# NSA attention branches of a transformer block: two of four heads' exponentials weighted on ScalarE in place of GpSimd

## The chip, the cores and the metric

One core of one Trainium2 chip runs the whole block as one program. The metric is the device time of one execution in microseconds (us). TensorE does the matmuls and transposes, VectorE (DVE in the profile) and ScalarE (ACT) work on SBUF and PSUM, GpSimd (POOL) on SBUF only, SyncE (SP) issues DMAs.

## The reference, cut to what matters

The block takes x (1024 tokens by 1024), projects it, runs two attentions (an NSA attention with three branches and a sliding-window attention with a sink), mixes them with gates, projects, and ends with an MLP. The change touches two branches of the NSA attention, "selected" and "window". For 2 groups of 4 heads, in 8 blocks of 128 queries, each branch computes

```python
e = jnp.exp(s - m)                                   # masked_softmax
p = e / jnp.maximum(jnp.sum(e, axis=-1, keepdims=True), 1e-30)
o_s = jnp.einsum('bgrqn,bgqnd->bqgrd', p_s, vg)       # selected branch
o_w = jnp.einsum('bgrqk,bkgd->bqgrd', p_w, vwc)       # window branch
return gs[..., 0:1] * oc + gs[..., 1:2] * o_s + gs[..., 2:3] * o_w
```

so a row of exponentials of one head is divided by its sum and multiplied by its gate: one factor per query (partition) and head. With 16 blocks of 64 keys in all and 16 to be chosen, the selected branch takes every earlier key.

## The kernel before, in words

All matmuls with full-size operands are made of three (high by high, high by low, low by high), since each float32 operand is split into two float32r parts. The helper `split` (L84) does that: a copy on ScalarE (L87) writes the high part, a subtraction on VectorE or GpSimd (L91) the low part.

The NSA stage stands in `nsa_units` (L635). A unit is one branch of one query block: for each group g (2) and block i (8) a window unit (rows of up to 640 keys, L687 to L702) and a selected unit (rows of 128 times i + 1 keys, up to 1024, L705 to L722). That makes 32 units in all. A unit has two parts.

- `scores` (L478): for each of 4 heads, two matmuls per chunk of keys into a PSUM bank (L489, L490), a VectorE instruction that adds the bias, negates and keeps the running minimum (L496), and an Exp on ScalarE that also sums (L502). Then `weights` makes one factor per query and head in three small VectorE instructions (L646 to L648, the last one multiplying by the gate). Last, the four rows are multiplied in place by their factors: heads 1 and 3 on GpSimd (L510), heads 0 and 2 on VectorE (L513). `POOL_N` (L42) holds the heads for GpSimd; the sliding-window stage has `POOL_S` (L41), all four.
- `attend` (L516): per 128 keys, four transposes on TensorE into a PSUM bank `pt` (L520), a split of it into `th` (ScalarE, L87) and `tl` (VectorE, L91), and two matmuls into the output bank, with `th` (L532) and `tl` (L533). `fill` (L414) puts matmuls of the gate projections (L124 to L126, tile `mm`) behind the transposes. Those projections have splits of weights of their own, with the low part on GpSimd (`wl`, L91), and evictions on ScalarE (`gst`, L205).

`merge` and `run` (L535, L549) interleave the `attend` steps of one unit with the `scores` steps of the next. The compressed branch (tile `ec`, L656 to L675) goes in front of each window unit. The order of the instructions on each engine is not the program's own: L1267 opens the program with `schedule_with_timeline_sim=True`, so a planner orders them when the program is built, by its own estimate of when each is ready. On the chip each engine then runs its list in that order.

Of the kernel before, what the change touches and what calls it, by code (L numbers as in the profile page):

```python
# [10 lines left out]
AF = mybir.ActivationFunctionType  # L11
# [5 lines left out]
T = 1024  # L17
# [15 lines left out]
HEAD = (0.5, 0, 0.25, 0, 0, 0, 0, 0)  # L33
# [5 lines left out]
FILL_S = 2.0  # L39
FILL_N = 1.0  # L40
POOL_S = (0, 1, 2, 3)  # L41
POOL_N = (1, 3)  # L42
TB = 2
NPAIR = 16
NPRE = 4
# [7 lines left out]
def tile_hybrid_block(ctx: ExitStack, tc: tile.TileContext, x, norm_mix_pre, norm_mix_post, norm_mlp_pre,  # L53
                      norm_mlp_post, w_in, cmp_pos_k, cmp_w1_k, cmp_w2_k, cmp_pos_v, cmp_w1_v, cmp_w2_v,
                      attn_sinks, rel_bias, w_up_nsa, w_up_swa, w_out, w_mlp_in, w_mlp_out, onehot, out):
    nc = tc.nc
# [3 lines left out]
    def pool(name, bufs=1, side="left", space=None):  # L60
        kw = {} if space is None else {"space": space}
        if space is not DRAM:
            kw["reuse_waits"] = "tile"
        if space is None:
            kw["side"] = side
        return tc.tile_pool(name=name, bufs=bufs, **kw)
# [74 lines left out]
    def rstd_of(tp, ss):  # L141


        s = tp.tile([P, 1], F32, name="rs_s", tag="rs_s", bufs=3)
        nc.scalar.activation(s, ss, AF.Sqrt, scale=0.25 / D, bias=eps_t)
        t = tp.tile([P, 1], F32, name="rs_t", tag="rs_t", bufs=3)
        nc.vector.tensor_scalar(t, ss, 0.25 / D, 0.25 * EPS, op0=ALU.mult, op1=ALU.add)
        r = tp.tile([P, 1], F32, name="rs_r", tag="rs_r", bufs=3)
        nc.vector.reciprocal(r, s)
        a = tp.tile([P, 1], F32, name="rs_a", tag="rs_a", bufs=3)  # L150
        nc.vector.scalar_tensor_tensor(a, r, t, s, op0=ALU.mult, op1=ALU.add)
        o = tp.tile([P, 1], F32, name="rs_o", tag="rs_o", bufs=3)
        nc.vector.reciprocal(o, a)
        return o
# [17 lines left out]
    with ExitStack() as s_u:  # L172
# [36 lines left out]
        with ExitStack() as s:  # L209
# [33 lines left out]
            with ExitStack() as s0:  # L243
# [28 lines left out]
                for b in range(NB):  # L272
# [11 lines left out]
                    r = rstd_of(tp, ss)  # L284
# [115 lines left out]
        with ExitStack() as s:  # L400
# [13 lines left out]
            def fill(amount, after=None):  # L414

                credit[0] += amount
                while credit[0] >= 1.0:
                    credit[0] -= 1.0
                    done[0] += 1
                    if after is None:  # L420
                        step()
                    else:
                        with tc.issue_after(after.ins):
                            step()
# [27 lines left out]
            def q_proj(qp, c0, tag, bufs):  # L452
                res = []
                for _ in q_steps(qp, c0, tag, bufs, res):
                    pass
                return res
# [18 lines left out]
                        nc.vector.tensor_tensor(kl[other, cs], kf[own, :], kh[own, cs].bitcast(F32), op=ALU.subtract)  # L475
                return res

            def scores(ep, etag, ew, qs, qcol, chunks, inits, res, weights, on_pool, extra=0.0):  # L478


                nm = ep.tile([P, 4], F32, name="nm", tag="nm", bufs=4)
                sm = ep.tile([P, 4], F32, name="sm", tag="sm", bufs=4)
                n = sum(c[2] for c in chunks)
                for r in range(4):
                    e = ep.tile([P, ew], F32, name="e", tag=etag, bufs=4)
                    prev, off = inits[r], 0
                    for ci, (kh, kl, w, bias) in enumerate(chunks):
                        ps = ps_s()
                        nc.tensor.matmul(ps[:, :w], qs[r][:, qcol], kh, start=True, stop=False)  # L489
                        mm = nc.tensor.matmul(ps[:, :w], qs[r][:, qcol], kl, start=False, stop=True)  # L490
                        fill(extra, mm)
                        if ci == len(chunks) - 1:
                            acc = nm[:, r:r + 1]
                        else:
                            acc = ep.tile([P, 1], F32, name="nm0", tag="nm0", bufs=4)
                        nc.vector.tensor_tensor_reduce(out=e[:, off:off + w], in0=ps[:, :w], in1=bias(r), scale=-1.0,  # L496
                                                       scalar=prev, op0=ALU.add, op1=ALU.min, accum_out=acc)
                        prev = acc
                        off += w
                        if ci < len(chunks) - 1:  # L500
                            yield
                    nc.scalar.activation(e[:, :n], e[:, :n], AF.Exp, scale=-1.0, bias=nm[:, r:r + 1],  # L502
                                         accum_out=sm[:, r:r + 1])
                    res.append(e)
                    if r < 3:
                        yield
                w = weights(nm, sm)
                for r in range(4):
                    if r in on_pool:
                        nc.gpsimd.tensor_tensor(res[r][:, :n], res[r][:, :n], w[:, r:r + 1].to_broadcast([P, n]),  # L510
                                                op=ALU.mult)
                    else:
                        nc.vector.tensor_scalar(res[r][:, :n], res[r][:, :n], w[:, r:r + 1], None, op0=ALU.mult)  # L513
                yield
# [59 lines left out]
            with ExitStack() as s0:  # L574
                qp = s0.enter_context(pool("swa"))
# [47 lines left out]
            with ExitStack() as s0:  # L623
                qp = s0.enter_context(pool("nsa"))
                for g in range(2):
# [4 lines left out]
                    qs = q_proj(qp, C_QN + g * 256, "q", 4)  # L630
                    qs = qs + q_proj(qp, C_QN + g * 256 + 128, "q", 4)
# [3 lines left out]
                    def nsa_units():  # L635
                        for i in range(NB):
                            qc = slice(i * P, (i + 1) * P)
                            kend = (i + 1) * P
                            y0 = 896 - P * i
                            ones = [1e30] * 4  # L640
                            o = []

                            def weights(br, i=i):
                                def f(nm, sm):
                                    w = qp.tile([P, 4], F32, name="w", tag="wgt", bufs=4)
                                    nc.vector.tensor_scalar(w, sm, 1e-30, None, op0=ALU.max)  # L646
                                    nc.vector.reciprocal(w, w)
                                    nc.vector.tensor_tensor(w, w, gsig[:, i, br, g * 4:g * 4 + 4], op=ALU.mult)  # L648
                                    return w
                                return f  # L650
# [3 lines left out]
                            ew = []  # L654
# [22 lines left out]
                            if i < 4:  # L677
                                k0 = 0
                                chunks = [(kwh[:, 0:kend], kwl[:, 0:kend], kend,
                                           lambda r, y0=y0: bn[:, r, y0:])]  # L680
                            else:
                                k0 = (i - 4) * P
                                k1 = k0 + 256
                                chunks = [(kwh[:, k0:k1], kwl[:, k0:k1], 256, lambda r: bfar[:, r, :]),
                                          (kwh[:, k1:kend], kwl[:, k1:kend], 384, lambda r: bn[:, r, 640:])]

                            def scores_a(i=i, qc=qc, ew=ew, chunks=chunks, cmp_scores=cmp_scores, weights=weights):  # L687
                                cmp_scores()
                                yield
                                yield from scores(qp, "ew", 640, qs, qc, chunks, ones, ew, weights(2), POOL_N, HEAD[i])  # L690

                            def attends_a(i=i, k0=k0, ec=ec, ew=ew, o=o):
                                o.append(ps_o())
# [3 lines left out]
                                for kb in range(k0 // P, i + 1):  # L697
                                    attend(qp, ew, kb * P - k0, P, o[0], vn[:, kb, 2 + g].rearrange("p a d -> p (a d)"),
                                           False, False, FILL_N)
                                    yield  # L700

                            yield scores_a(), 1 + 4 * len(chunks), attends_a(), i + 2 - k0 // P  # L702


                            chunks = []  # L705
                            n = kend if i < 4 else kend // 2
# [3 lines left out]
                            es = []  # L710

                            def attends_b(i=i, es=es, o=o):
                                for kb in range(i + 1):
                                    attend(qp, es, kb * P, P, o[0], vn[:, kb, g].rearrange("p a d -> p (a d)"),
                                           False, kb == i, FILL_N)
                                    if kb < i:
                                        yield
                                put_o(o[0], g * 256, i)
                                yield

                            yield (scores(qp, "es", T, qs, qc, chunks, ones, es, weights(1), POOL_N, HEAD[i]), 4 * len(chunks),
                                   attends_b(), i + 1)  # L722

                    run(nsa_units(), 1)
            s_pv.close()
            s_ot = ctx.enter_context(ExitStack())
# [13 lines left out]
    with ExitStack() as s:  # L740
# [58 lines left out]
        ep = s_e.enter_context(pool("etmp"))  # L799
# [472 lines left out]
```

## Time and profile before

| what | value |
|---|---|
| time, 3 runs | 1577.01 us median, 1576.17 to 1580.71 |
| the profiled execution's own time | 1580.5 us |
| its span in the profile | 1578.7 us |
| mean granted clock of TensorE | 0.981 of full speed |
| busy: TensorE, VectorE, ScalarE, GpSimd | 94%, 69%, 48%, 28% of the span |

The time of an execution is a little longer than the span, which runs from the first instruction to the last. Times in the rows are us from the start of the span, durations of single instructions in the views by line are ns. In a row of the timeline, a bracket gives the time the engine was idle just before, and what ended that; "x2" means that two instructions are merged in one row. NSA units run between 300 and 690 us.

### The profile page before, as it was taken

What the parts mean: (1) busy time and instruction counts of PE and PEld (TensorE: products, weight loads), DVE (VectorE), ACT (ScalarE), POOL (GpSimd) and SP (SyncE); (2) the same over time, 40 slices, a digit from 0 to 9 for tenths busy, and PEclk for the clock granted to TensorE, in tenths of its full rate; (3) what the DMA queues carried; (4) which work ended last, traced back from release to release, by engine and by line L of the source; (5) the groups of instructions that cost most, each with busy time, mean ns of one, the idle gap of its engine ahead of it and who ended that gap; (6) DMA issues with size and microseconds to landing.
All of it is one profiled execution on the core that took longest, in us unless ns stands there. A gap on an engine that the chain in (4) does not pass through costs nothing. (4 is left out here: it accounts for less than half of the span.)

```text
span 1578.7 us, 20103 instructions
## 1 busy us (share of the span) xinstructions
PE 1487.3 (94%) x6920; PEld 1214.2 (77%) x6920; DVE 1088.4 (69%) x2086; ACT 751.2 (48%) x1461; POOL 439.8 (28%) x354
## 2 busy tenths in 40 slices
PE   6998999999899999999988978999999899999997
PEld 5897888878777777778866766778888688888886
DVE  5455775598964998836537787877757566594775
ACT  5343675576653766653336563332222334334543
POOL 3000351132310232231133014867555410000302
PEclk9999999999999999999999998999999999999999
DMA  7733125111132111164256652444443598263451
GB/s 201 256 103 82 38 51 154 41 44 31 34 97 51 47 34 31 34 225 139 94 186 229 225 159 58 158 162 156 147 153 134 208 336 302 94 188 118 150 184 54
DMA packets 162038, 204.79 MB, mean 130 GB/s; under 512 B 15120, under 2 KB 105264, under 8 KB 161936
## 3 DMA queue, kind: packets, MB, share of 16 engines
q1 hardware_dynamic: 154224, 180.68, 36.5%
q0 software_dynamic: 6992, 20.48, 3.7%
q10 hardware_dynamic: 720, 2.36, 0.4%
q8 instruction: 54, 0.88, 0.2%
q14 instruction: 48, 0.39, 0.1%
HBM read 153.02 MB, written 58.32 MB: 134 GB/s over the span
## 5 line engine op out<-in xcount | busy, mean ns | idle before, releaser
L124 PE MATMUL mm<-uh,wh 128*128 128x512 f32 x464 | 201.4, 434 | 4.1 <-DVE qb L448 3.2
L510 POOL TENSOR_TENSOR e<-e,w 128x256 f32<-128x256 f32 (+7 forms) x128 | 111.6, 898 | 286.4 <-DVE w L648 148.9
L125 PE MATMUL mm<-ul,wh 128*128 128x512 f32 x464 | 184.9, 398 | 0.0
L126 PE MATMUL mm<-uh,wl 128*128 128x512 f32 x464 | 184.5, 398 | 0.0
L87 ACT ACTIVATE th<-pt 128x512 fp32r<-128x512 f32 (+1 forms) x178 | 105.1, 593 | 95.0 <-PE pt L520 84.9
L502 ACT ACTIVATE e<-e,nm 128x256 f32<-128x256 f32 (+7 forms) x192 | 124.4, 649 | 36.8 <-DVE nm L496 36.4
L91 DVE TENSOR_TENSOR tl<-pt,th 128x512 fp32r<-128x512 f32 x162 | 110.0, 682 | 33.8 <-ACT th L87 32.7
L87 ACT ACTIVATE fh<-fraw 128x1024 fp32r<-128x1024 f32 x56 | 59.4, 1062 | 145.3 <-PE xs L1165 78.3
L87 ACT ACTIVATE wh<-wraw 128x1024 fp32r<-128x1024 f32 x69 | 73.0, 1058 | 111.1 <-PE mm L125 36.7
L91 DVE TENSOR_TENSOR fl<-fraw,fh 128x1024 fp32r<-128x1024 f32 x56 | 69.2, 1241 | 78.2 <-ACT fh L87 78.2
L520 PE MATMUL pt<-ident,e 128*128 128x128 f32 x648 | 104.8, 276 | 1.9 <-DVE e L513 0.9
L1165 PE MATMUL xs<-vl,fh 128*128 128x512 f32 x256 | 100.7, 393 | 4.2 <-DVE vl L91 4.2
L126 PEld LDWEIGHTS mm<-uh,wl 128*128 128x128 f32 x464 | 88.0, 190 | 20.9
L124 PEld LDWEIGHTS mm<-uh,wh 128*128 128x128 f32 x464 | 88.9, 192 | 17.4 <-issue 3.3
L91 DVE TENSOR_TENSOR wl<-wraw,wh 128x1024 fp32r<-128x1024 f32 x53 | 69.0, 1301 | 45.9 <-ACT wh L87 45.5
L1165 PE MATMUL xs<-vh,fl 128*128 128x512 f32 x256 | 100.5, 393 | 0.0
L1165 PE MATMUL xs<-vh,fh 128*128 128x512 f32 x256 | 100.2, 392 | 0.0
L1188 POOL TENSOR_TENSOR cc<-cc,gB 128x512 f32<-128x512 f32 x14 | 24.3, 1759 | 269.0 <-ACT sq L1187 267.3
L520 PEld LDWEIGHTS pt<-ident,e 128*128 128x128 f32 x648 | 81.7, 141 | 22.7 <-issue 2.5
L125 PEld LDWEIGHTS mm<-ul,wh 128*128 128x128 f32 x464 | 89.0, 192 | 12.0
L116 POOL TENSOR_TENSOR wl<-wraw,wh 128x384 fp32r<-128x384 f32 (+2 forms) x26 | 38.7, 1493 | 161.7 <-ACT wh L108 161.7
L91 POOL TENSOR_TENSOR wl<-wraw,wh 128x1024 fp32r<-128x1024 f32 x16 | 38.6, 2410 | 159.5 <-ACT wh L87 159.5
(286 smaller groups left out, 4086.0 us busy)
## 6 DMA issues: line engine op xcount, KB each, us to landing
fraw<-f_d SPq DMA_DIRECT2D x48, 512.0 KB, 3.6
wraw<-in_w_mlp_in_dram SPq DMA_DIRECT2D x36, 512.0 KB, 4.5
wraw<-in_w_out_dram SPq DMA_DIRECT2D x32, 512.0 KB, 3.6
f_d<-q SPq DMA_DIRECT2D x64, 256.0 KB, 3.6
b<-in_w_mlp_out_dram SPq DMA_DIRECT2D x32, 512.0 KB, 10.8
wraw<-in_w_in_dram SPq DMA_DIRECT2D x27, 512.0 KB, 4.7
f_d<-c SPq DMA_DIRECT2D x48, 256.0 KB, 4.0
gate_d<-gst SPq DMA_DIRECT2D x32, 256.0 KB, 2.1
```

Source lines behind the costliest of these rows:

```text
L87: nc.scalar.activation(h, src, AF.Copy)
L91: eng.tensor_tensor(l, src, h.bitcast(F32), op=ALU.subtract)
L116: eng.tensor_tensor(lv[:, a:b], rv[:, a:b], hv[:, a:b].bitcast(F32), op=ALU.subtract)
L124: nc.tensor.matmul(ps, ah, bh, start=first, stop=False)
L125: nc.tensor.matmul(ps, ah, bl, start=False, stop=False)
L126: nc.tensor.matmul(ps, al, bh, start=False, stop=last)
L502: nc.scalar.activation(e[:, :n], e[:, :n], AF.Exp, scale=-1.0, bias=nm[:, r:r + 1], accum_out=sm[:, r:r + 1])
L510: nc.gpsimd.tensor_tensor(res[r][:, :n], res[r][:, :n], w[:, r:r + 1].to_broadcast([P, n]), op=ALU.mult)
L520: tr = nc.tensor.transpose(pt[:rows, r, :], es[r][:, off:off + rows], ident)
L1165: nc.tensor.matmul(bank[t], l_[:, j, ts], r_[:, j, :], start=a_, stop=z_, skip_group_check=True)
L1188: (nc.vector if b == NB - 1 else nc.gpsimd).tensor_tensor(cc[:, ns], cc[:, ns], gB[:, ns], op=ALU.mult)
```

## The change

`scores` gets a second set, `on_act`. A head in it is multiplied on ScalarE as a Copy whose scale is the factor of each partition. The two calls in the NSA stage pass heads 1 and 3 there and nothing for GpSimd; the call in the sliding-window stage still passes its four heads for GpSimd.

```diff
-POOL_N = (1, 3)
+ACT_N = (1, 3)
...
-            def scores(ep, etag, ew, qs, qcol, chunks, inits, res, weights, on_pool, extra=0.0):
+            def scores(ep, etag, ew, qs, qcol, chunks, inits, res, weights, on_pool=(), extra=0.0, on_act=()):
...
                 w = weights(nm, sm)
                 for r in range(4):
-                    if r in on_pool:
+                    if r in on_act:
+                        nc.scalar.activation(res[r][:, :n], res[r][:, :n], AF.Copy, scale=w[:, r:r + 1])
+                    elif r in on_pool:
                         nc.gpsimd.tensor_tensor(res[r][:, :n], res[r][:, :n], w[:, r:r + 1].to_broadcast([P, n]),
                                                 op=ALU.mult)
                     else:
...
-                                yield from scores(qp, "ew", 640, qs, qc, chunks, ones, ew, weights(2), POOL_N, HEAD[i])
+                                yield from scores(qp, "ew", 640, qs, qc, chunks, ones, ew, weights(2), extra=HEAD[i], on_act=ACT_N)
...
-                            yield (scores(qp, "es", T, qs, qc, chunks, ones, es, weights(1), POOL_N, HEAD[i]), 4 * len(chunks),
+                            yield (scores(qp, "es", T, qs, qc, chunks, ones, es, weights(1), extra=HEAD[i], on_act=ACT_N), 4 * len(chunks),
                                    attends_b(), i + 1)
```

## Rows read from the trace of the kernel before

**Rows 1.** The page: TensorE over the whole span (busy us, share, instructions).
```profile
PE 1487.3 (94%) x6920; PEld 1214.2 (77%) x6920; DVE 1088.4 (69%) x2086; ACT 751.2 (48%) x1461; POOL 439.8 (28%) x354
```

**Rows 2.** Busy time by stretch: the NSA stage, then what follows it.
```profile
core 0: us, PE busy (x) PEld busy (x) DVE busy (x) ACT busy (x) POOL busy (x), PEclk, DMA share, GB/s
300.00:690.00 390.00, 366.93 (x1964) 301.03 (x1963) 319.20 (x941) 244.64 (x600) 104.55 (x76) 0.99 0.17 47
...
690.00:795.00 105.00, 105.00 (x462) 86.26 (x460) 57.98 (x73) 44.36 (x51) 18.62 (x12) 1.00 0.48 161
```

**Rows 3.** Waits of TensorE, 300 to 690 us: total, times, longest.
```profile
PE o L533 <- DVE tl L91: 15.3, 14, 2.0
PE s L489 <- DVE nm L496: 4.7, 4, 2.1
...
PE pt L520 <- DVE e L513: 0.9, 3, 0.3
PE pt L520 <- POOL e L510: 0.3, 1, 0.3
```

**Rows 4.** Timeline of TensorE around one of those waits.
```profile
401.60 0.60 PE L520 MATMUL pt<-ident,e 128*128 128x128 f32 x4
...
402.98 0.40 PE L532 MATMUL o<-th,vn 128*128 128x512 f32 x1
405.41 0.50 PE L533 MATMUL o<-tl,vn 128*128 128x512 f32 x1 [2.04 <-DVE tl L91]
```

**Rows 5.** Timeline of VectorE, the same stretch.
```profile
400.81 0.16 DVE L648 TENSOR_TENSOR w<-w,gsig 128x4 f32<-128x4 f32 x1
...
401.31 3.45 DVE L513 TENSOR_SCALAR e<-e,w 128x768 f32<-128x768 f32 x2
404.68 0.68 DVE L91 TENSOR_TENSOR tl<-pt,th 128x512 fp32r<-128x512 f32 x1
```

**Rows 6.** Timeline of GpSimd, the same stretch.
```profile
401.13 3.21 POOL L510 TENSOR_TENSOR e<-e,w 128x768 f32<-128x768 f32 x2 [10.07 <-DVE nm L668]
```

**Rows 7.** Timeline of ScalarE, the same stretch.
```profile
401.27 0.58 ACT L87 ACTIVATE th<-pt 128x512 fp32r<-128x512 f32 x1
...
402.75 0.58 ACT L87 ACTIVATE th<-pt 128x512 fp32r<-128x512 f32 x1
```

**Rows 8.** L513: all 64 (ns min/median/max), and two with no GpSimd instruction ahead.
```profile
L513 DVE TENSOR_SCALAR e<-e,w x64: 276/966/2385, 308.1 to 669.4; 128x640 f32<-128x640 f32 x20, 128x128 f32<-128x128 f32 x8, 128x256 f32<-128x256 f32 x8, 128x384 f32<-128x384 f32 x8
...
L513 DVE TENSOR_SCALAR e<-e,w x1: 473/473/473, 345.1 to 345.1; 128x512 f32<-128x512 f32 x1
...
L513 DVE TENSOR_SCALAR e<-e,w x1: 752/752/752, 668.2 to 668.2; 128x1024 f32<-128x1024 f32 x1
```

**Rows 9.** Busy time of L513 alone, then of L510 alone, in the NSA stage.
```profile
300.00:690.00 390.00, 62.51 (x64) 0.99 0.17 47
...
300.00:690.00 390.00, 76.17 (x64) 0.99 0.17 47
```

**Rows 10.** ScalarE by line and shape, 300 to 690 us (busy us, mean ns | idle before).
```profile
L87 ACT ACTIVATE th<-pt 128x512 fp32r<-128x512 f32 x132 | 77.9, 593 | 81.9 <-PE pt L520 75.9 <-DVE nm L496 4.9 <-PE o L527 0.3
L502 ACT ACTIVATE e<-e,nm 128x640 f32<-128x640 f32 x40 | 33.0, 827 | 8.7 <-DVE nm L496 8.5
...
L87 ACT ACTIVATE wh<-wraw 128x1024 fp32r<-128x1024 f32 x14 | 14.7, 1052 | 14.4 <-PE mm L125 14.4
...
L502 ACT ACTIVATE e<-e,nm 128x1024 f32<-128x1024 f32 x8 | 9.2, 1145 | 0.9 <-DVE nm L496 0.9
```

**Rows 11.** Line L502, 100 to 690 us: its table loads.
```profile
L502 ACT ACT_TABLE_LOAD  x1: 1283/1283/1283, 149.7 to 149.7; - x1
```

**Rows 12.** Timelines of VectorE, ScalarE and GpSimd around another long wait.
```profile
332.75 1.73 DVE L513 TENSOR_SCALAR e<-e,w 128x384 f32<-128x384 f32 x2
334.40 2.35 DVE L646 TENSOR_SCALAR w<-sm 128x4 f32<-128x4 f32 x1
...
332.83 1.05 ACT L87 ACTIVATE wh<-wraw 128x1024 fp32r<-128x1024 f32 x1
...
332.39 1.87 POOL L510 TENSOR_TENSOR e<-e,w 128x384 f32<-128x384 f32 x2 [5.30 <-PE pt L520]
334.23 2.50 POOL L91 TENSOR_TENSOR wl<-wraw,wh 128x1024 fp32r<-128x1024 f32 x1
```

**Rows 13.** Timelines of VectorE, ScalarE and TensorE in a unit without such a wait.
```profile
442.50 0.16 DVE L648 TENSOR_TENSOR w<-w,gsig 128x4 f32<-128x4 f32 x1
...
442.98 0.60 ACT L87 ACTIVATE th<-pt 128x512 fp32r<-128x512 f32 x1 [0.93 <-PE pt L520]
...
443.64 0.39 PE L532 MATMUL o<-th,vn 128*128 128x512 f32 x1
```

## The prediction, made before the result was known

> **What bounds the kernel now.** I read the page first: TensorE is busy 94% of the span, the others far less [rows 1]. So time is won only where TensorE stands idle, and lost only where it is made to. Then the busy time by stretch: in the NSA stage, 300 to 690 us, TensorE is busy 366.9 of 390 us, VectorE 319.2, ScalarE 244.6; in the 105 us behind it TensorE has no idle time at all [rows 2]. What the stage wins therefore moves the rest of the program forward undiminished, and it can win at most 390 - 366.9 = 23.1 us. Third, who TensorE waits for there [rows 3]: 14 waits for `tl`, 15.3 us; 4 for a minimum, 4.7 us; 4 for the weighted exponentials themselves, 1.2 us.
>
> Fourth, the timelines around one of the 14. TensorE's L532 takes `th` at 402.98, then stands 2.04 us until L533 gets its `tl` [rows 4]. That `tl` starts at 404.68, though its `th` was written from 401.27 to 401.85 [rows 5, 7]. In between VectorE is inside its two L513 for 3.45 us [rows 5], while GpSimd runs its two L510 from 401.13 for 3.21 us [rows 6]. All 14 waits look like this: one or both L513 stand ahead of the `tl`, and an L510 overlaps them in nearly all.
>
> L513 is slow because of L510. Where no GpSimd instruction was ahead, 512 columns took 473 ns and 1024 took 752 ns, while the longest of the 64 took 2385 ns [rows 8]. Those two give 194 ns + 0.545 ns a column, so 612 ns for 768 columns, against half of 3.45 us. The 3.45 us end with the 3.21 us of GpSimd: the second L513 gets through only when GpSimd is nearly done.
>
> **The change part by part.** Each unit loses two L510 on GpSimd, 64 in all, 76.2 us of GpSimd's time [rows 9], and gets two Copies on ScalarE. The 64 instructions have 33,792 columns (20 of 640, 8 each of 128, 256, 384 and 512, 4 each of 768, 896 and 1024).
>
> VectorE: its own 64 L513 have the same widths. Uncontended they take 64 x 0.194 + 33,792 x 0.000545 = 12.4 + 18.4 = 30.8 us in place of 62.5 us [rows 8, 9], so VectorE gets back 31.7 us, about 1 us per unit, just where `tl` queues.
>
> ScalarE: the trace has no Copy with a scale read from SBUF. Below it lies the plain Copy, 1052 ns for 1024 columns; above it the Exp, which reads a bias from SBUF, 827 ns for 640 and 1145 ns for 1024 [rows 10]. I take the Exp's price, since both read one value per partition: 297 ns + 0.828 ns a column, 64 x 0.297 + 33,792 x 0.000828 = 47.0 us; 93 ns less each gives 41.0 us. ScalarE has 390 - 244.6 = 145 us idle, so it can hold them. No table load is added: the 192 Exps ran among Copies behind a single load of 1.28 us [rows 11].
>
> A multiply on ScalarE is dearer than on VectorE: by the Exp's row 827 ns for 640 columns, against 194 + 640 x 0.545 = 543 ns. The Trainium skill (ScalarE: Activation LUTs, Rules for kernel authors) says to do multiplications on VectorE and not on ScalarE. By that rule heads 1 and 3 would go to VectorE too, at 30.8 us more there, about what the end of the contention frees, and this change would be the wrong one. What that would make of the time is the second rival.
>
> The new wait: a unit's two Copies need the factor (L648) and stand in ScalarE's queue, with the next `th` behind them. They are a burst of 1.47 us on average (47.0 / 32): 0.8 us for rows of 128, 1.65 for 640, 2.3 for 1024; some 0.1 us less per Copy, as neighbours overlap. `tl` needs `th`, so VectorE and then TensorE wait. Where the planner puts the Copies among the `th` is not to be seen before it is built, so each term has two ends, Copies first and `th` first.
>
> - **The five long waits** (rows of 768 and 896 twice each, 1024 once; 9.6 us): in the one shown, Copies first move its `th` by some 1.6 us, `tl` ends near 404.2 and L533 starts 1.1 us earlier than 405.41; with `th` first VectorE is free by 402.5 and the whole 2.0 us go. In the same way 0.7 to 1.8 us at 896 and 0.3 to 1.8 at 1024. Together 2 x 1.1 + 2 x 0.7 + 0.3 = 3.9 to 9.6 us; I take 7, since ScalarE is idle 37% of the stage and part of the Copies will find it so.
> - **The nine shorter ones** (5.7 us): rows of 256, 512 and 640, one of 1024, where the burst is about as long as the L513 it replaces, so 0 to 5.7; I take 2.5, nearer the low end for that reason.
> - **Two of the four waits for a minimum** are 2.06 us each: L646, the next factor, stands 2.35 us on VectorE while GpSimd splits a weight for 2.50 us [rows 12]. GpSimd began that only when its L510 were done, at 334.23. Afterwards both L513 (384 columns, 403 ns) end near 333.5 and L646 can run before the weight's split, which needs `wh`, written until 333.88 or later. Two waits, 0 to 4.1 us; I take 3.
> - **Waits for the weighted rows**: for 768 columns GpSimd's second result comes at 404.34, 3.4 us behind the factor [rows 5, 6]; two Copies would take 1.8. 0 to 1.2 us; I take 0.5.
> - **New waits in the 15 units without one** (32 less the 14 and three with waits for the weighted rows): in the one shown the factor is ready at 442.66, `th` runs from 442.98 to 443.58, and its L532 starts at 443.64 [rows 13]: no slack. A burst first would cost 1.2 us there, 18 us over 15 units; `th` first costs nothing. A `th` comes every 3.0 us (132 in 390 us [rows 10]), so about half of the bursts meet one, with half of 1.47 us left: 15 x 0.5 x 0.74 = 5.5 us. The planner sees ScalarE's load and can move some, so I take 4.
>
> GpSimd's remaining work (the weights' splits) only comes earlier. SP's DMAs are untouched in number. The sum: 7 + 2.5 + 3 + 0.5 - 4 = 9 us faster; its ends are 20.6 us faster and 3.9 - 18 = 14 us slower. It is made in an execution of 1580.5 us (span 1578.7), 3.5 us above the median of 1577.0; taken from the median it gives 1568.
>
> **The rivals.** First, **the queue moves from VectorE to ScalarE**: Copies come first in most units, the long waits shrink by only 4 us, the short ones stay, and new waits of about 4 us balance it: 1577, no change. For it speaks that L532 follows `th` without slack [rows 13]; against it that ScalarE is idle 37% of the stage and VectorE 18% [rows 2]. Chance 0.25.
>
> Second, **slower: ScalarE's bursts stand on TensorE's path**. In the chain L520, `th`, L532 each Copy ahead of a `th` is time of TensorE. If 28 of the 47.0 us (60%) come out as waits and the freed ones are 13 us (7 + 2.5 + 3 + 0.5), it is 15 us slower, 1592. It decides from 13 us of new waits on, 28% of the bursts. For it speaks the same row; against it that ScalarE stood idle 81.9 us ahead of its `th`, 75.9 of them for TensorE [rows 10]. The rule cited above points this way. Chance 0.11.
>
> Third, **nothing replaces the waits**: all freed waits go and the planner finds room for the bursts, 1556.4. Chance 0.1, a part of "faster".
>
> That the change doesn't do what it says, say a Copy costing far more than an Exp, I leave in the second: at twice the price the bursts are 94 us, within ScalarE's 145 idle, but hardly clear of `th`.
>
> **How the numbers follow.** A measurement can tell 0.3%, 4.7 us, from no change. The forecast has 0.54, with the third rival 0.64 for faster by more; same 0.25; slower 0.11. The range reaches from near the best end, 1558, to just past the first rival, 1578; its own middle part is 1562 to 1572. It leaves out the second rival and a little at the low end.
>
> **What would show it.** L513 at some 550 ns for 640 columns and near 31 us in all; no L510 between 300 and 690 us; Copies near 830 ns for 640 columns on ScalarE and its busy time in the stage near 290 us; TensorE's waits for `tl` behind L513 gone, with some waits for `th` in their place; the L646 of 2.35 us gone. It is wrong if the idle time of TensorE in the stage stays at 23 us or grows with waits that lead to ScalarE, or if L513 stays long without L510.

## The result, and the profile after

The changed kernel takes 1551.68 us (median of 4 runs, 1550.25 to 1553.9), the kernel before beside it 1576.85 (4 runs, 1576.17 to 1580.71): ratio 0.984, interval 0.9816 to 0.9857. A second set of runs gave 0.9833. So it is 25.2 us faster: the sign was right, the 9 us forecast were not, and 1551.7 lies below the whole range.

In the changed kernel L513 has become L515 and L648 L650; L520, L532 and L533 are L522, L534 and L535. L510 is now the Copy on ScalarE. First the busy time by stretch. The stretch of the NSA stage is cut so that it ends as far behind the stage's last matmul as in [rows 2].

```profile
core 0: us, PE busy (x) PEld busy (x) DVE busy (x) ACT busy (x) POOL busy (x), PEclk, DMA share, GB/s
298.00:664.00 366.00, 360.26 (x1966) 298.18 (x1965) 285.88 (x941) 281.79 (x664) 28.50 (x12) 1.00 0.18 50
664.00:769.00 105.00, 104.95 (x461) 86.12 (x459) 58.09 (x74) 44.12 (x51) 18.51 (x12) 1.00 0.48 162
```

The stage takes 366 us in place of 390; the 105 us behind it are as long as before. TensorE's idle time in it fell from 23.1 us (390 - 366.9, [rows 2]) to 5.7. Its busy time fell too, from 366.9 to 360.3 us, for the same matmuls, and the granted clock stands at 1.00 for 0.99. So 17.3 us of the 24 are waits and 6.7 are matmuls that ran shorter. The profiled spans differ by 30.2 us (1578.7 and 1548.5), 5 more than the medians, since that execution of before lies 3.7 us above its median here and this one 1.4 below. Of the 30.2 us, 24.4 lie in the stage (396.4 and 372.0 us from its first matmul to its last), 1.8 ahead of it and 4.0 behind.

Next TensorE's waits in the stage (us in total, times, longest), against [rows 3]:

```profile
PE o L529 <- DVE th L91: 1.7, 2, 0.9
PE o L535 <- DVE tl L91: 1.4, 5, 0.3
...
PE s L489 <- DVE nm L496: 0.6, 2, 0.3
```

The waits for `tl` went from 15.3 to 1.4 us, those for a minimum from 4.7 to 0.6, those for weighted rows from 1.2 to none. No wait leads to the Copies. One pair is new, L529's, 1.7 us: a matmul of the compressed branch that waits for VectorE's part of its `th`. The first of the two stops begins at 307.0 us, a microsecond ahead of the first Copy.

The weighted multiplications themselves, on VectorE (ns min/median/max) and on ScalarE (busy us, mean ns | idle before), with the `th` on ScalarE:

```profile
L515 DVE TENSOR_SCALAR e<-e,w x64: 281/516/753, 306.4 to 644.9; 128x640 f32<-128x640 f32 x20, 128x128 f32<-128x128 f32 x8, 128x256 f32<-128x256 f32 x8, 128x384 f32<-128x384 f32 x8
```

```profile
L87 ACT ACTIVATE th<-pt 128x512 fp32r<-128x512 f32 x132 | 77.1, 592 | 39.8 <-PE pt L522 36.7 <-PE o L529 2.2 <-DVE nm L496 0.3
...
L510 ACT ACTIVATE e<-e,w 128x640 f32<-128x640 f32 x20 | 15.5, 824 | 0.8 <-DVE w L650 0.8
```

The longest VectorE multiplication fell from 2385 ns [rows 8] to 753. A Copy costs what an Exp of its width does [rows 10]. ScalarE's idle time ahead of its `th` was spent: 81.9 us before, 39.8 now.

Last the unit of [rows 4 to 7], in the changed kernel on VectorE, ScalarE and TensorE:

```profile
392.26 1.15 DVE L515 TENSOR_SCALAR e<-e,w 128x768 f32<-128x768 f32 x2
393.32 0.68 DVE L91 TENSOR_TENSOR tl<-pt,th 128x512 fp32r<-128x512 f32 x1
```

```profile
392.50 0.58 ACT L87 ACTIVATE th<-pt 128x512 fp32r<-128x512 f32 x1
...
393.31 1.75 ACT L510 ACTIVATE e<-e,w 128x768 f32<-128x768 f32 x2
394.96 1.07 ACT L87 ACTIVATE th<-pt 128x512 fp32r<-128x512 f32 x2
```

```profile
393.94 0.40 PE L534 MATMUL o<-th,vn 128*128 128x512 f32 x1
394.17 0.40 PE L535 MATMUL o<-tl,vn 128*128 128x512 f32 x1
```

The two multiplications take 1.15 us in place of 3.45, `tl` starts right behind them, and L535 follows an L534 without a gap where L533 stood 2.04 us [rows 4]. The first `th` went ahead of the Copies, the next ones behind them.

### The profile page after: what moved, and what is told of

Its sections match the earlier page's. It is cut to its first block, busy times and chain, and to the rows that moved or that the text cites. A ratio compares the mean times of both kernels' runs of the same rounds, so it can differ in the third digit from the quotient of the medians.

```text
span 1548.5 us, 19945 instructions
## 1 busy us (share of the span) xinstructions
PE 1475.5 (95%) x6920; PEld 1208.1 (78%) x6920; DVE 1053.7 (68%) x2086; ACT 788.3 (51%) x1525; POOL 362.6 (23%) x290
## 4 chain that ended last, share of the span: by engine, by line
PE 69%; issue 8%; DVE 6%; POOL 3%; DMA 2%; ACT 2%; DVEq 0%; POOLq 0%; ACTq 0%
PE xs L1167 10%; PE ys L1167 8%; PE mm L124 5%; PE mm L126 5%; PE mm L125 5%; PE ps L959 5%; PE ps L961 5%; PE ps L960 5%; PE pt L522 5%; PE o L535 2%; PE o L534 2%; PE s L489 2%; DMA wraw<-in_w_out_dram 2%; PE s L490 2%; PE ps L124 2%
## 5 line engine op out<-in xcount | busy, mean ns | idle before, releaser
L502 ACT ACTIVATE e<-e,nm 128x256 f32<-128x256 f32 (+7 forms) x192 | 124.3, 649 | 20.0 <-DVE nm L496 19.5
L522 PE MATMUL pt<-ident,e 128*128 128x128 f32 x648 | 101.1, 273 | 0.3 <-DVE tl L91 0.2
L522 PEld LDWEIGHTS pt<-ident,e 128*128 128x128 f32 x648 | 80.7, 140 | 18.4 <-issue 0.9
L1190 POOL TENSOR_TENSOR cc<-cc,gB 128x512 f32<-128x512 f32 x14 | 24.3, 1762 | 268.9 <-ACT sq L1189 267.2
L87 ACT ACTIVATE ws_h<-wraw 128x512 fp32r<-128x512 f32 x48 | 30.1, 629 | 107.1 <-PE ps L960 104.8
L959 PE MATMUL ps<-bh,ws_h 128*128 128x512 f32 x192 | 76.3, 397 | 3.9 <-ACT ws_h L87 1.7
```

The source lines that it names most:

```text
L87: nc.scalar.activation(h, src, AF.Copy)
L522: tr = nc.tensor.transpose(pt[:rows, r, :], es[r][:, off:off + rows], ident)
L959: nc.tensor.matmul(ps, ah[:, k, :], bh[i][:, k, :], start=n[0], stop=False, skip_group_check=True)
```

## The experiments

The theory is **contention**: GpSimd's multiplications held up VectorE's, and `tl` queued behind. Its rivals are **order** (the planner's new order brings the gain), **load** (VectorE or ScalarE simply has less to do), and, on the price side, whether ScalarE's bursts are hidden. Each edit is to the changed kernel unless another is named. The table is worked out from the traces. "Stage" runs from the first matmul of the compressed scores to the last output matmul; "idle" sums TensorE's stops over 80 ns in it; "half" is its time at half the granted clock in it; "mult." is VectorE's busy time in weighted multiplications. "Stage", "idle", "half" and "mult." are of one execution each, the profiled one.

```
kernel                          median us  stage  idle  half  mult.
before                          1576.85    396.4  22.9  10.2  62.5
changed                         1551.68    372.0   5.5   0    28.7
e3  + GpSimd work               1574.98    394.7  19.9   6.8  60.8
e12   only rows >= 768          1565.09    384.4  15.4   3.4  41.1
e13   only rows <= 640          1562.58    381.9  12.0   0    50.9
e8  before, GpSimd heads 0, 2   1577.83    397.9  22.5  10.2  62.1
e1  all on VectorE              1557.65    377.8  10.8   0    54.9
e6  three VectorE, one ScalarE  1553.01    371.5   7.1   0    42.1
e4  GpSimd and ScalarE          1568.48    387.6  15.4   3.4   0
e10 ScalarE's bursts doubled    1568.73    388.6  16.0   0    28.7
e5  all on ScalarE              1584.85    405.6  20.2  13.7   0
```

**e3, GpSimd's work put back.** GpSimd multiplies as much as before (rows cut at 896 columns), but of the bias, into a tile that nothing reads, so the output stays as it was.

```diff
                 w = weights(nm, sm)
+                for r in on_act:
+                    m = min(n, 896)
+                    nc.gpsimd.tensor_tensor(junk_n[0][:, :m], bnow[0][:, r, :m], w[:, r:r + 1].to_broadcast([P, m]),
+                                            op=ALU.mult)
                 for r in range(4):
```

> The changed kernel with 64 GpSimd multiplications of the old sizes (896 columns in place of 1024) put back at the old place, from the bias tile into a scratch tile that nobody reads. TensorE, VectorE and ScalarE run the changed kernel's lists in its order. Theory 'contention' (L513 was long because it waited inside for GpSimd, and that made tl late): the multiplications on VectorE grow from about 31 back to about 60 us in the NSA stage, TensorE stops for tl by 13 to 18 us, time 1568 to 1580. Rival 'order' (the gain is the new order of the three lists, and the rows ready earlier): stays at 1552, within 3 us.

It took 1574.98 us, 0.9988 of before (0.9973 to 1.0003): 23.3 of the 25.2 us are lost again. TensorE, VectorE and ScalarE have the changed kernel's lists here, instruction for instruction, so the order alone is worth next to nothing. TensorE's waits in the stage, and one of them on the timelines of VectorE, GpSimd and TensorE (L519 is the multiplication, L539 takes `tl`):

```profile
PE o L539 <- DVE tl L91: 5.8, 10, 1.8
PE s L489 <- DVE nm L496: 5.4, 9, 1.8
PE pt L526 <- DVE e L519: 2.6, 5, 0.7
```

```profile
456.12 2.84 DVE L519 TENSOR_SCALAR e<-e,w 128x1024 f32<-128x1024 f32 x2
458.88 1.27 DVE L91 TENSOR_TENSOR tl<-pt,th 128x512 fp32r<-128x512 f32 x2
...
456.23 4.27 POOL L510 TENSOR_TENSOR junk_n<-bn,w 128x896 f32<-128x896 f32 x2 [16.20 <-DVE w L657]
...
459.61 0.50 PE L539 MATMUL o<-tl,vn 128*128 128x512 f32 x1 [1.78 <-DVE tl L91]
```

VectorE's two instructions take 2.84 us, where two of 1024 columns alone take 1.5 (753 ns is the longest in the changed kernel), and `tl` and TensorE are late behind them, though nothing reads GpSimd's result. Both halves of the theory stand in this one timeline. One number was missed: 13 to 18 us of waits for `tl` were expected, 5.8 came. The other stops stand at other results of VectorE's queue: the minimum (5.4), the weighted rows (2.6), VectorE's part of `th` and the tile `osb` (2.1 and 1.8, not shown). Of the 22.7 us by which the stage is longer, 14.4 are stops and 3.4 the halved clock; the other 4.9 were not traced to a cause.

**e12 and e13, the same for a part of the rows.** `for r in on_act if n >= 768 else ():` in the loop above, then `if n <= 640`.

> As e3_lock_back, but GpSimd's scratch multiplications only in the six units with rows of 768 columns or more; TensorE, VectorE and ScalarE again run the changed kernel's lists. Theory 'contention': the stops of e3 in those units come back (about 9 us in e3's trace), and with stops of 1.8 us also one to three stretches of 3.4 us at half TensorE clock in the stage, 1.7 us each: 1560 to 1567. Rival 'clock by chance' (the half-clock stretches have nothing to do with the stops): the same stops, but as many stretches as the changed kernel, none: 1559 to 1562.

> As e3_lock_back, but GpSimd's scratch multiplications only in the 26 units with rows of 640 columns or fewer, the rest of e3's. If the waits of units add up, it costs what e12 left of e3's loss, some 10 us: 1558 to 1565. Theory 'the clock falls behind long stops': e3's stops in these units are 1.1 us at most, so no stretch at half clock in the stage; rival 'clock by chance': one to three as before.

They took 1565.09 us (0.993, 0.9907 to 0.9954) and 1562.58 (0.9899, 0.9876 to 0.9921): 13.4 and 10.9 us worse than the changed kernel, together 24.3 against 23.3 of e3. The cost adds up, and the 12 long instructions hold more than half of it; but the short rows matter too. TensorE's waits for `tl` are 6 of 7.0 us in all with the long rows (the longest 2.2), and 10 of 3.1 us with the short ones (0.5). On the clock, e13's profile has no half-clock stretch, as its theory said. e12's has one, behind a stop of 1.7 us, and none behind its two of 2.2 us; its time lies in the theory's range, but its four runs spread over 7 us, so the time alone doesn't decide between the two ranges.

**e8, another order on the kernel before.** `POOL_N = (0, 2)` in place of `(1, 3)`: the same contention, another order.

> The kernel before the change with heads 0 and 2 on GpSimd and 1 and 3 on VectorE: the same work on the same engines, in an order of its own. Theory 'contention': 1573 to 1580. Rival 'order' (any new order could have given the gain): it moves by 5 us or more.

1577.83 us, 1.0003 (0.999 to 1.0016): no gain. With e3 the order falls.

**e1, all four heads on VectorE.** No GpSimd, no ScalarE.

```diff
-ACT_N = (1, 3)
+ACT_N = ()
```

> The changed kernel with all four heads multiplied on VectorE, none on ScalarE or GpSimd. VectorE's 128 multiplications take about 62 us uncontended, so VectorE is as busy in the stage as before the change (about 319 us). Theory 'contention': no long multiplication, so most of the gain stays, 1550 to 1562. Rival 'load' (VectorE was too full and ScalarE's idle time was what paid): 1570 or more, as VectorE is as full as before.

1557.65 us, 0.9889 (0.9866 to 0.9911). VectorE does twice as many multiplications as before, in less time (54.9 us for 128 against 62.5 for 64), and 19 us of the gain are there without ScalarE. So it isn't VectorE's smaller load that brings most of it. What is left to ScalarE is 6 us, as TensorE's waits in the stage show:

```profile
PE o L535 <- DVE tl L91: 5.6, 10, 1.6
PE s L489 <- DVE nm L496: 2.7, 4, 1.1
```

**e6, one head on ScalarE.** `ACT_N = (3,)`.

> Three heads on VectorE, head 3 on ScalarE, none on GpSimd. Theory 'contention': no long multiplication, so it lies between the changed kernel (1552) and all four on VectorE (1558), or a little below both as the ScalarE bursts are halved: 1549 to 1557. Rival 'load': VectorE has 15 us more than in the changed kernel, 1557 or more.

1553.01 us, 0.9854 (0.9839 to 0.9869), stage 371.5: the same as the changed kernel. Between one and two heads the split doesn't matter.

**e4, GpSimd and ScalarE, nothing on VectorE.**

```diff
-ACT_N = (1, 3)
+ACT_N = (0, 2)
+POOL_N = (1, 3)
```

(with `POOL_N` passed again in the two calls).

> Heads 1 and 3 on GpSimd as before the change, heads 0 and 2 on ScalarE, none on VectorE. Theory 'contention': only the small factor instructions of VectorE can meet GpSimd, the gain stays, 1550 to 1562. Rival 'late rows' (before the change GpSimd's second row came 3 us behind its factor, and TensorE's order had to be built around that): 1570 or more.

It missed: 1568.48 us, 0.9949 (0.9932 to 0.9965), short of the rival's range too, and no wait of TensorE leads to GpSimd's rows. No weighted multiplication is left on VectorE, yet TensorE waits for its minimum. VectorE's and GpSimd's timelines around two of these waits (lines are one higher than in the changed kernel):

```profile
PE s L490 <- DVE nm L497: 8.1, 10, 2.1
```

```profile
334.54 2.56 DVE L678 TENSOR_TENSOR ec<-ec,w 128x256 f32<-128x256 f32 x1
...
334.44 2.38 POOL L92 TENSOR_TENSOR wl<-wraw,wh 128x1024 fp32r<-128x1024 f32 x1
...
426.14 1.39 DVE L651 TENSOR_TENSOR w<-w,gsig 128x4 f32<-128x4 f32 x1
...
427.79 0.41 DVE L678 TENSOR_TENSOR ec<-ec,w 128x256 f32<-128x256 f32 x1
...
424.19 3.32 POOL L513 TENSOR_TENSOR e<-e,w 128x896 f32<-128x896 f32 x2 [12.54 <-DVE w L651]
```

The same L678 takes 0.41 us alone and 2.56 beside a GpSimd instruction of 2.38; a product of 128x4, 0.16 us in the changed kernel, takes 1.39 beside GpSimd's weighted multiplications. So VectorE's instructions with two SBUF inputs are held up as well, and taking only the multiplications off VectorE is not enough. The Trainium skill (SBUF — State Buffer, section "SBUF: two separate sides") calls the port pair of the two engines an exclusive lock, which whichever starts first holds for its whole instruction. These rows agree: 334.54 + 2.56 us is 0.28 us past the end of GpSimd's, and 426.14 + 1.39 is 0.02 past the end of the other.

**e5, all four heads on ScalarE.** `ACT_N = (0, 1, 2, 3)`.

> All four heads on ScalarE, none on VectorE or GpSimd: ScalarE gets another 47 us in bursts twice as long. Theory 'bursts are hidden' (the order puts them where no th is due): 1550 to 1558. Rival 'bursts stand on TensorE's path' (28% of them or more come out as waits): 1565 or more, with waits of TensorE for th or tl behind ScalarE.

The theory missed and the rival's range holds: 1584.85 us, 1.0051 (1.0033 to 1.0068), slower than before, with no weighted multiplication left on VectorE or GpSimd. TensorE's waits in the stage, and the longest kind of them on ScalarE and TensorE:

```profile
PE o L534 <- ACT th L87: 7.2, 6, 2.4
PE o L535 <- DVE tl L91: 4.9, 13, 1.2
PE pt L522 <- ACT e L510: 3.6, 6, 0.7
```

```profile
354.67 2.55 ACT L510 ACTIVATE e<-e,w 128x512 f32<-128x512 f32 x4
357.12 0.58 ACT L205 ACTIVATE gst<-mm 128x512 f32<-128x512 f32 x1
357.59 1.06 ACT L87 ACTIVATE th<-pt 128x512 fp32r<-128x512 f32 x2
...
358.23 0.50 PE L534 MATMUL o<-th,vn 128*128 128x512 f32 x1 [2.04 <-ACT th L87]
```

This is the mechanism of the prediction's second rival, at twice the burst: four Copies ahead of a `th`, and TensorE stands 2.04 us.

**e10, the changed kernel's bursts doubled.** After the loop ScalarE multiplies again, of the bias, into a tile that nothing reads, so the output stays as it was.

```diff
+                for r in on_act:
+                    m = min(n, 896)
+                    nc.scalar.activation(junk_n[0][:, :m], bnow[0][:, r, :m], AF.Copy, scale=w[:, r:r + 1])
```

> The changed kernel with two more Copies per unit on ScalarE, from the bias tile into a scratch tile that nobody reads: ScalarE has the load and the bursts of e5_all_scalar, but the rows are ready as early as in the changed kernel. If e5 was slow because th stands behind long bursts: 1568 to 1588, with waits of TensorE for th or tl. If e5 was slow because its rows were ready late: 1552 to 1560.

1568.73 us, 0.9952 (0.9936 to 0.9969): 17 us worse than the changed kernel. TensorE never waits for a weighted row in it; what stands out is the `th` behind the burst:

```profile
PE o L537 <- ACT th L87: 5.9, 8, 1.2
PE o L538 <- DVE tl L91: 5.8, 16, 0.7
```

The stage is 16.6 us longer than the changed kernel's, 10.5 of it stops. The planner gave e10 an order of its own on TensorE, VectorE and ScalarE, so, other than in e3, the order isn't held still. e5's stage is 33.6 longer; doubled bursts alone would be about half of that, and in e5 come 13.7 us at half clock (6.9 us lost) and 3.6 us of waits for the weighted rows. That leaves some 6 us of e5 open.

**e14, the sliding-window stage off GpSimd as well.** Its call passes `()` for `POOL_S` and `ACT_N` as `on_act`.

> The changed kernel with the sliding-window stage's four multiplications moved off GpSimd too: heads 1 and 3 to ScalarE, heads 0 and 2 to VectorE. In that stage VectorE had no multiplication to be held up, so theory 'contention' gives little: 1546 to 1554. If GpSimd's slowness by itself costs time there, 1545 or less; if ScalarE or VectorE becomes too full there, 1556 or more.

1558.99 us, 0.989 (0.9876 to 0.9905), 7 us worse than the changed kernel. The NSA stage is as long as in the changed kernel (372.0 us); the stretch ahead of it, in the changed kernel and then in e14, is 6 us longer:

```profile
140.00:287.00 147.00, 141.58 (x721) 117.07 (x720) 97.59 (x270) 89.29 (x233) 42.58 (x67) 0.99 0.32 81
```

```profile
140.00:293.00 153.00, 143.03 (x722) 117.71 (x721) 103.91 (x303) 100.01 (x265) 7.20 (x3) 0.98 0.31 79
```

There GpSimd does all four heads and VectorE none, and moving its 35 us to the others adds 4.5 us to TensorE's idle time (147 - 141.6 = 5.4, then 153 - 143.0 = 10.0). The waits that grew there are for VectorE, which now has multiplications ahead of its other work: for `tl` from 0.2 to 2.5 us, for `osb` from none to 1.9.

**The changed kernel again**, beside the others.

> The changed kernel once more, beside e13 and e8 on the same chip: 1550 to 1554, no stretch at half clock in the NSA stage.

1551.97 us, 0.9833 (0.9814 to 0.9852). None of the versions tried beats the changed kernel; e6 equals it.

## Why the prediction was right about the contention and wrong about the new wait and the size

Right were the bound (TensorE's idle time in the NSA stage), the cause (L510 stretches L513, `tl` queues behind, TensorE stands), and the prices: 28.7 us of VectorE against 30.8 forecast, Copies of 824 ns against 827. The five signs named under "What would show it" came, but for the waits for ScalarE's `th` that were to take the place of some: none did. One reading was too wide: in two of the 14 waits (0.7 us each, at 322.0 and 532.2 us of before) both L513 took 341 ns, with no GpSimd instruction beside them. The L646 of 2.35 us went as argued; it now takes 0.15 us and runs ahead of the weight's split (VectorE, then GpSimd):

```profile
330.81 0.15 DVE L648 TENSOR_SCALAR w<-sm 128x4 f32<-128x4 f32 x1
...
332.79 2.43 POOL L91 TENSOR_TENSOR wl<-wraw,wh 128x1024 fp32r<-128x1024 f32 x1 [29.94 <-ACT wh L87]
```

**The step that failed** is the new wait: "the factor is ready at 442.66, `th` runs from 442.98 to 443.58, and its L532 starts at 443.64 [rows 13]: no slack", put at -4 us, with an end of -18. That L532 isn't the one which reads this `th`. It reads the `th` before, written from 440.44 on, as more rows of the same unit show (ScalarE, VectorE, TensorE, in the kernel before):

```profile
440.44 0.60 ACT L87 ACTIVATE th<-pt 128x512 fp32r<-128x512 f32 x1
...
444.63 0.68 DVE L91 TENSOR_TENSOR tl<-pt,th 128x512 fp32r<-128x512 f32 x1
...
444.10 0.39 PE L533 MATMUL o<-tl,vn 128*128 128x512 f32 x1
...
445.47 0.39 PE L532 MATMUL o<-th,vn 128*128 128x512 f32 x1
```

The `tl` made from the `th` of 442.98 starts at 444.63, when the L533 of 444.10 is already running, so the pair at 443.64 and 444.10 is of the step before. The `th` of 442.98 is read at 445.47: it lies for 1.9 us where the prediction had 0.06. The one unit read as having no slack had more than an average burst of 1.47 us, and the price of 1.2 us there, 18 us over 15 units, rested on it. In the changed kernel the same unit has the burst first and the `th` behind it, and no stop (ScalarE, then TensorE):

```profile
427.30 1.55 ACT L510 ACTIVATE e<-e,w 128x640 f32<-128x640 f32 x2 [0.22 <-DVE w L650]
428.85 0.60 ACT L87 ACTIVATE th<-pt 128x512 fp32r<-128x512 f32 x1
```

```profile
428.21 0.60 PE L522 MATMUL pt<-ident,e 128*128 128x128 f32 x4
...
429.35 0.39 PE L534 MATMUL o<-th,vn 128*128 128x512 f32 x1
...
430.96 0.40 PE L534 MATMUL o<-th,vn 128*128 128x512 f32 x1
```

The burst ends at 428.85, just as the transposes of 428.21 are done (428.81), so it holds up this `th` by 0.04 us. The L534 of 429.35 again belongs to the step before; this `th` is read at 430.96, since TensorE's list has gate matmuls, the earlier step's pair and the next step's transposes in between. Over the 148 transpose steps of the stage (132 of the window and selected units, 16 of the compressed branch), the k-th `th` paired with the k-th transposes and the k-th matmul, the lags are, worked out from the traces (mean us):

```
                              before  changed  e10   e5
transposes' end to th start   0.53    0.66     0.99  1.17
th end to its matmul          1.90    1.71     1.52  1.44
```

So even before, a `th` lay 1.9 us on average until its matmul (median 1.51; 1.63 on average over the 132), more than the 1.47 us of an average burst, though 55 of the 148 had less. That could have been counted from the trace of before. The changed kernel draws 0.2 us of it. The slack is finite: e10 doubles the bursts and pays 17 us, e5 more. The same premise, that a burst ahead of a `th` delays TensorE, held the other terms down. By the sum's terms, in us:

```
term                              forecast  measured
waits for tl, long and short         9.5      13.9   (15.3 to 1.4)
waits for a minimum                  3         4.1   (4.7 to 0.6)
waits for the weighted rows          0.5       1.2
new waits                           -4        -1.7   (L529; none for the Copies)
sum of the waits                     9        17.5
matmuls that ran shorter             0         6.7
```

Of the 15 us that were missed, 8.5 are in the waits and 6.7 in the last line. The waits alone, taken from 1577, give 1559.5, inside the range; the last line, put at nothing, is what carries the time below it.

**The missing term** is that last line, the second step that failed. "It can win at most 390 - 366.9 = 23.1 us" took TensorE's busy time as fixed; it isn't, and the stage won 24. One of three stretches of 20 us of before with a granted clock of 0.91 (the others are 330 to 350 and 610 to 630 us), and the same two instructions at both of the clock's levels (2.4 and 1.2 GHz), with the stop between. They start 0.23 us apart at the one and 0.43 at the other:

```profile
430.00:450.00 20.00, 18.16 (x94) 15.03 (x93) 16.94 (x41) 9.77 (x19) 4.89 (x3) 0.91 0.15 42
```

```profile
430.43 0.39 PE L125 MATMUL mm<-ul,wh 128*128 128x512 f32 x1
430.66 0.39 PE L126 MATMUL mm<-uh,wl 128*128 128x512 f32 x1
...
433.11 0.50 PE L533 MATMUL o<-tl,vn 128*128 128x512 f32 x1 [1.83 <-DVE tl L91]
...
435.26 0.63 PE L125 MATMUL mm<-ul,wh 128*128 128x512 f32 x1
435.69 0.63 PE L126 MATMUL mm<-uh,wl 128*128 128x512 f32 x1
```

In each the clock is halved for 3.4 us (together 10.2, at half speed 5.1 us lost), and that begins 2.5 to 3.2 us after the start of a stop of about 2 us. The remaining 1.6 of the 6.7 us fit with the first matmuls after a stop, which take longer (0.50 us for L533 here, 0.40 in the gapless run), and with fewer stops over 80 ns (16 in place of 28); they were not counted one by one. The changed kernel's stage has none of these stretches. The 5.1 us are of one execution, but the unprofiled ones point the same way: by their granted clocks on record (one less the mean clock, times the span, an estimate) the 36 executions of before beside the experiments lose 29 us to the lower level over the whole program, the eight of the changed kernel 24.

Of the rivals, "nothing replaces the waits" was nearest: its 1556.4, less the 5.1 us of clock, would be 1551.3. It had a chance of 0.1. That it comes so near is partly luck: not all waits went (1.4 us for `tl` and 0.6 for a minimum are left), L529's 1.7 us are new, and the clock was no part of it. The rule of the Trainium skill cited there (ScalarE: Activation LUTs, Rules for kernel authors), to multiply on VectorE and not on ScalarE, agrees with the runs only in part: all on VectorE (e1) is 6 us slower than half on ScalarE, all on ScalarE (e5) 33 us slower.

## What to carry to other kernels

When GpSimd and VectorE overlap on SBUF, look at the same instruction's shortest and longest time, and at what stands behind the longest in its queue: the cost is there, not in GpSimd's busy time. Before pricing a burst on another engine, count the slack of its neighbours over all steps (end of the producer to start of its consumer), not in one. Pair each producer with its own consumer: where steps overlap, the next matmul of that line in the timeline can be the step before's, and a third instruction (here `tl`) tells which it is. Here a burst within that slack cost TensorE nothing, and doubled bursts cost 17 us. And removing stops of a busy TensorE can win more than their length: here 17 us of stops went and 24 us with them, some 5 of the difference by the granted clock.

## What the runs showed of the hardware that was not expected

- VectorE's products with two SBUF inputs are held up by GpSimd as much as those with a factor per partition: 128x4 from 0.16 to 1.39 us, 128x256 from 0.41 to 2.56 (e4). The subtraction that writes `tl` has one input in PSUM and isn't: in e3 two of them took 1.27 us (458.88) while GpSimd was busy from 456.23 to 460.50, and one alone takes 0.68.
- The granted clock falls to half for 3.4 us behind some of TensorE's stops. Before had seven stops of 1.8 to 2.1 us, and the clock fell behind three of them (336.2, 431.3 and 613.0 us), not behind the others (403.4, 460.9, 546.4 and 642.0). The changed kernel, e1, e6, e10, e13 and e14, whose longest stop is 1.6 us, had no such stretch in the stage. But e12 had one behind a stop of 1.7 us and none behind its two of 2.2, e5 had two behind stops of 0.6 and 1.1 us in all besides its two behind stops of 2 us and more, and e8 one behind stops of 1.5 us in all. So the length of the stop alone does not settle it, and what does stays open.
